# One conditioning pass behind each low part of weights, and four more pairs of tiles turned by transfers

## The chip, the cores and the metric

The kernel runs on one core of a Trainium2 chip. The time is the device time of one execution in microseconds (us); lower is better. The engines are named as in the profile: PE multiplies matrices (PEld is its weight load), DVE and ACT work element by element, POOL and SP here mostly issue transfers, and 16 DMA engines carry them.

## The reference

One decoder layer in float32, 256 tokens of width 2048, with two feed-forward parts around a token mixing:

```python
c_act = jax.nn.silu(c)
mod = (c_act @ w_ada[l] + b_ada[l]).reshape(b, N_MOD, D_MODEL)          # 9 x 2048
h = modulate(rms_norm(x, norm_ffn1[l]), mod[:, 0], mod[:, 1])
x = x + 0.5 * mod[:, 2][:, None, :] * swiglu(h, w_ffn1_gu[l], w_ffn1_down[l])
h = modulate(rms_norm(x, norm_mix[l]), mod[:, 3], mod[:, 4])
x = x + mod[:, 5][:, None, :] * token_mixing(h, w_in[l], w_ret_branch[l], w_swa_branch[l], w_out[l], sinks[l])
h = modulate(rms_norm(x, norm_ffn2[l]), mod[:, 6], mod[:, 7])
x = x + 0.5 * mod[:, 8][:, None, :] * swiglu(h, w_ffn2_gu[l], w_ffn2_down[l])
return rms_norm(x, norm_final)
```

`swiglu` multiplies by `w_gu` (2048 x 11264), forms silu(gate) * up (256 x 5632) and multiplies by `w_down`. `token_mixing` multiplies by `w_in` (2048 x 13312), runs a chunked retention and a sliding-window attention, multiplies each by a 2048 x 2048 branch matrix, gates and adds the two, and multiplies by `w_out` (2048 x 2048). The vector `mod` is the conditioning: a product of one row, c_act, with the whole of `w_ada` (2048 x 18432).

## The kernel before, in words

*Weights.* A matrix comes 1 MB at a time: `load` (L326) takes one of four buffers of the pool `raws` and issues the transfer on SP (L328). One such buffer holds two halves of 128 x 1024. `split` (L347) makes of each half a high part on ACT (L351, `wh`) and a low part on DVE (L353, `wl`), in a pool with three buffers of each. `products` (L331) then runs three matmuls for each of 4 column blocks of the activations: L338 high by high, L339 activations' low part by the weights' high part, L341 by the weights' low part. A low part is thus followed by 12 matmuls. In `gemm_part` (L390) each half ends with `tick()`, each 1 MB with `turn_step()`. L386 and L387 make high and low parts of activations in the same way.

*Conditioning.* The product with `w_ada` is done on DVE, not on PE: a row of 128 x 2048 (1 MB, `ada_load`, L201) is multiplied by silu(c) and summed in four passes of 512 columns (L206, `ada_pass`), each an instruction of DVE with a short one that reads the sum. `conditioning` (L243) is a generator that does one pass at each step, and issues a row's load some passes ahead (`pace["ahead"]`). `tick` advances it by `pace["rate"]` passes for each low part. The row sits in a buffer of `raws` too (`raw_row`) in the last group of the opening, in the mixing and in the second feed-forward part, and in half a slot (`two_rows`) in the rest of the first one. Three sets are done this way: 3 x 16 rows within the first feed-forward part, 3 x 16 within the mixing, 16 within the second feed-forward part.

*The opening.* The first 16 products of the first feed-forward part (pairs 0 to 7 of a gate and an up block) are done in four groups of inner blocks, L1009, while x is being normalised; in the last group each pair ends in `swiglu_up` (L657).

*Turning.* The result of a pair (two tiles of 128 x 512) must be transposed before the next product. `transpose_to` (L475) does it with four transposes on PE (L479) and a copy (L480, on ACT) for each tile. `turn_by_dma` (L486) does it without PE: two copies on ACT that lay the 16-bit halves apart (L496), a transposing transfer on SP (L501), two copies on ACT that put them together (L512); `later` (L613) spreads these over the next `turn_step`s.

*Order.* SP issues in the order of the program. On PE, DVE and ACT a scheduler orders the instructions by its own model of their times, except where the code is under a manual schedule. `tc.issue_after(ins)` forbids it to put an instruction ahead of `ins` on the same engine. `low[-1]` and `cast[-1]` are the newest low and high part, `pace["behind"]` is set by weights that are split by hand ahead of a stage (L469).

Of the kernel before, what the change touches and what calls it, by code (L numbers as in the profile page):

```python
# [20 lines left out]
DFF = 5632  # L21
# [3 lines left out]
CH = 512  # L25
# [3 lines left out]
EARLY = 8  # L29
# [48 lines left out]
def layer_kernel(  # L78
# [40 lines left out]
    def nm(s):  # L119
        uid[0] += 1  # L120
        return f"{s}_{uid[0]}"
# [16 lines left out]
    def slot():  # L138
        return slots.tile([P, KD * S], F32, tag="slot", name=nm("slot"))
# [55 lines left out]
    AQ = 4  # L195

    def ada_load(m, k, w, loads=1):
        src = w_ada[(m * KD + k) * P : (m * KD + k + 1) * P, :]
        for i in range(loads):
            at = slice(i * D // loads, (i + 1) * D // loads)  # L200
            nc.sync.dma_start(w[:, at], src[:, at])  # L201

    def ada_pass(k, w, sums, q, passes=AQ):

        at = slice(q * D // passes, (q + 1) * D // passes)
        nc.vector.tensor_tensor_reduce(  # L206
            out=w[:, at],
            in0=w[:, at],
            in1=cact[:, at],
            scale=1.0,  # L210
            scalar=0.0,
            op0=ALU.mult,
            op1=ALU.add,
            accum_out=sums[:, k, q : q + 1],
        )

    def ada_sums():
        return two.tile([P, KD, AQ], F32, tag="sums", name=nm("sums"))

    def ada_end(m, ks, sums, i=None, passes=AQ):  # L220

        dest = modc[:, m, ks]
        nc.vector.tensor_reduce(out=dest, in_=sums[:, ks, :passes], axis=AX.X, op=ALU.add)
        nc.vector.tensor_add(dest, dest, bcols[:, m, ks])
        if i is not None:
            nc.vector.tensor_mul(dest, dest, gains[:, i, ks])
# [16 lines left out]
    def conditioning(outputs, place, behind):  # L243


        tiles = [(m, k) for m, _, _ in outputs for k in range(KD)]
        held = {}
        step = 0
        for m, gain, row in outputs:
            sums = ada_sums()  # L250
            for k in range(KD):
                for q in range(AQ):
                    for i in range(step // AQ, min((step + pace["ahead"]) // AQ + 1, len(tiles))):
                        if i not in held:
                            held[i] = place()
                            ada_load(*tiles[i], held[i])
                    if behind is not None and step < 2 * AQ:
                        with tc.issue_after(behind.ins):
                            ada_pass(k, held[step // AQ], sums, q)
                    else:  # L260
                        ada_pass(k, held[step // AQ], sums, q)
                    step += 1
                    if k == KD - 1 and q == AQ - 1:
                        ada_end(m, slice(0, KD), sums, gain)
                        if row is not None:
                            gate_out(m, row)
                    yield

    def gate_out(m, row):

        ps = bank()
        nc.tensor.transpose(ps[:KD, :P], modc[:, m, :], ident)
        flat = t512()[:KD, :P]
        nc.scalar.mul(flat, ps[:KD, :P], row)
        nc.gpsimd.dma_start(gate_d[m // 3].rearrange("(k p) -> k p", p=P), flat)
# [6 lines left out]
    def gate_load(row, m):  # L282
        return nc.gpsimd.dma_start(row, gate_d[m // 3][None, :].broadcast_to([P, D]))
# [4 lines left out]
    def set_pace(outputs, halves, place, ahead):  # L288
        assert next(pace["steps"], None) is None
        pace["steps"] = conditioning(outputs, place, pace["behind"])  # L290
        pace["rate"] = len(outputs) * KD * AQ / halves
        pace["due"] = 0.0
        pace["ahead"] = ahead
# [9 lines left out]
    def turn_step():  # L303

        for one_turn in list(turns):
            if next(one_turn, turns) is turns:
                turns.remove(one_turn)
# [49 lines left out]
    cast, low, newest = [], [], []  # L357
# [49 lines left out]
    def gemm(act, w, col0s, KT=KD, ahead=None):  # L407
        banks = [[acc_bank() for _ in range(NT)] for _ in col0s]
        for kb in range(KT // KB):
            gemm_part(act, w, col0s, banks, kb, KT, None if kb else ahead)  # L410
            step()
        return banks
# [244 lines left out]
    def swiglu_up(banks_g, banks_u, tiles, ci, parts=None, by_dma=False):  # L657

        k0 = ci * KB
        dest = tiles[k0 // KD].rearrange("p (k s) -> p k s", s=S)  # L660
        kk = k0 % KD
        work = []
        for t in range(NT):
            s = t512()
            g, u = banks_g[t], banks_u[t]
            if parts is not None:
                nc.vector.tensor_add(s, g, parts[0][t])
                nc.vector.tensor_add(parts[1][t], u, parts[1][t])
                g, u = s, parts[1][t]
            nc.scalar.activation(s, g, AF.Silu)  # L670
            nc.vector.tensor_mul(s, s, u)  # L671
            if by_dma:
                work.append(turn_by_dma(dest[:, kk : kk + KB, t * P : (t + 1) * P], s))
                continue
            transpose_to(
                dest[:, kk : kk + KB, t * P : (t + 1) * P],
                lambda j: s[:, j * P : (j + 1) * P],
                KB,
            )
        if work:  # L680
            turns.append(later(work))

    def ffn_up(held, w, tiles, first, bg=None, turned=(), ahead=None):
        for ci in range(first, DFF // CH):
            bg = bg or gemm(held, w, [ci * CH])[0]
            bu = gemm(held, w, [DFF + ci * CH], ahead=ahead)[0]
            swiglu_up(bg, bu, tiles, ci, by_dma=ci in turned)
            bg = ahead = None
# [194 lines left out]
    gu, dn = w_ffn1_gu[0], w_ffn1_down[0]  # L883
    held = Held()
    part = [slot() for _ in range(3)]
    tiles = [slot(), part[0]]
# [3 lines left out]
    behind = [[back.tile([P, CH], F32, tag="back", name=nm("back")) for _ in range(NT)] for _ in range(2)]  # L890

    def part_of(n):
        if n < 2:
            return behind[n]
        if n >= 14:
            return [beside[n - 14][:, t, :] for t in range(NT)]
        at = ((n - 2) % 4) * NT * CH
        return [part[(n - 2) // 4][:, at + t * CH : at + (t + 1) * CH] for t in range(NT)]
# [7 lines left out]
    def place(m, k):  # L906
        if k < 1:
            rows_of[m, k] = raw_row()
        else:
            ring.append(ring.pop(0))  # L910
            rows_of[m, k] = ring[-1]
        ada_load(m, k, rows_of[m, k], 2 if k < 2 else 1)
# [80 lines left out]
    def to_parts(n):  # L993
        for p, b in zip(part_of(n), banks.pop(n)):
            if n in moved:
                nc.vector.tensor_add(p, p, b)  # L996
            else:
                nc.scalar.copy(p, b)
        moved.add(n)
# [9 lines left out]
    for g, ks in enumerate(groups):  # L1009
        final = g == len(groups) - 1  # L1010
        if final:
            set_pace(ROWS_FFN1, 32 * 192 // 32, place_row, 1)
        order = chunks if (len(groups) - g) % 2 else chunks[::-1]
        coming = iter(()) if final else group(groups[g + 1])
        due = 0 if final else 2 * len(groups[g + 1])
        stay = () if final else order[-2:]
        for i, n in enumerate(order):
            visit(n, ks, n not in stay, final)
            if final:
                turn_step()  # L1020
            last = len(order) - 2
            for _ in range((i + 1) * due // last - i * due // last if i < last else i == last):
                next(coming, None)
            if n in stay:
                continue
            if not final:
                to_parts(n)
            elif n % 2:
                swiglu_up(
                    banks.pop(n - 1),  # L1030
                    banks.pop(n),
                    tiles,
                    n // 2,
                    (part_of(n - 1), part_of(n)),
                    n // 2 in (1, 5),
                )
    gate = gate_row()
    tiles.append(slot())
    row_ring.append(two_rows())
    pace["rate"] = (192 - 32) / 117  # L1040
    pace["ahead"] = AQ
    ffn_up(held, gu, tiles, EARLY, turned=range(EARLY, DFF // CH - 1))
    gate_in = gate_load(gate, 2)
    wi = w_in[0]
    held, head, ahead, *calls = into_norm(3, wi, O_SK, O_SV)
# [336 lines left out]
    gate = gate_row()  # L1382
    tiles = [slot() for _ in range(3)]
    set_pace([(8, None, 0.5)], 160, raw_row, 2)
    ffn_up(held, w_ffn2_gu[0], tiles, 0, head, range(DFF // CH - 1), ahead)
    gf = one.tile([P, KD * S], F32, tag="hh", name="gf")[:, :D]
    spare = one.tile([P, 2, KD * P], F32R, tag="hl", name="spare")
    nc.gpsimd.dma_start(gf, norm_final[None, :].broadcast_to([P, D]))
# [107 lines left out]
```

## Time and profile before

| | us |
|---|---|
| median of three runs (lowest, highest) | 2388.58 (2387.45, 2389.75) |
| profiled execution | 2393.78 |
| its span, first to last instruction | 2392.0 |
| PE busy in it | 2351.4 (98%) |
| DVE busy | 1702.1 (71%) |
| ACT busy | 1310.0 (55%) |
| mean granted clock of TensorE | 0.997 |

Durations are read from the profiled execution. A group's row gives the line, the engine, the operation, what it writes and reads, how often, its busy time in us and the mean of one in ns, and the engine's idle time just before with what ended it. In the trace the passes of L206 are called CUSTOM_DVE_ANT_0, and the short instruction behind each DVE_READ_ACCUMULATOR2_ANT; in the order rows both are ISA. Names of buffers carry no numbers in the trace.

### The profile page before, as it was taken

Reading aid. Unit: us, or ns where it says so; the run is one execution under the profiler, and the core shown is the slowest. Engines: PE = TensorE matmul, PEld = TensorE weight load, DVE = VectorE, ACT = ScalarE, POOL = GpSimd, SP = SyncE. Lnnn points to the kernel's source line nnn. Section 1 sums busy time; section 2 is a strip of 40 time slices with the busy share of each in tenths; the row PEclk is TensorE's granted clock in tenths of the full one; section 3 lists DMA queues with packets and bytes.
Section 4 is the critical chain, followed back from the end, with each engine's and each line's share of the span. In section 5 each row is a group of like instructions: output and inputs, shape, how many; then the busy total and the mean of one; then the engine's idle time right before and its main releaser. Section 6 shows DMA issues by size and latency. Waiting matters only on the chain. (4 is left out here: it accounts for less than half of the span.)

```text
span 2392.0 us, 28418 instructions
## 1 busy us (share of the span) xinstructions
PE 2351.4 (98%) x10470; PEld 1924.5 (80%) x10470; DVE 1702.1 (71%) x2635; ACT 1310.0 (55%) x1792; POOL 7.7 (0%) x18
## 2 busy tenths in 40 slices
PE   7999999999999999999999999999999999999998
PEld 5788888888788888778887787887888888888886
DVE  6887799778877768976776676767655555545656
ACT  6553456454546568774555464466445445454544
POOL 0000000000000000000000000000000000000000
PEclk9999999999999999999999999999999999999999
DMA  9977789998876789867689797755667877765553
GB/s 354 367 278 277 265 284 342 349 339 316 321 255 236 279 270 247 253 213 286 248 278 293 236 299 282 272 195 192 237 238 237 254 247 246 255 220 194 183 204 124
DMA packets 177581, 625.78 MB, mean 262 GB/s; under 512 B 100321, under 2 KB 100705, under 8 KB 106913
## 3 DMA queue, kind: packets, MB, share of 16 engines
q1 hardware_dynamic: 175362, 613.11, 74.4%
q0 software_dynamic: 1504, 9.81, 1.0%
q8 instruction: 82, 1.34, 0.2%
q10 hardware_dynamic: 576, 1.05, 0.1%
q14 instruction: 57, 0.47, 0.1%
HBM read 597.16 MB, written 4.22 MB: 251 GB/s over the span
## 5 line engine op out<-in xcount | busy, mean ns | idle before, releaser
L351 ACT CAST wh<-raw 128x1024 fp32r<-128x1024 f32 x794 | 834.0, 1053 | 927.1 <-PE pa L339 895.4
L353 DVE TENSOR_TENSOR wl<-raw,wh 128x1024 fp32r<-128x1024 f32 x794 | 964.2, 1223 | 524.6 <-ACT wh L351 522.3
L338 PE MATMUL pa<-wh,hh 128*128 128x512 f32 x2192 | 855.4, 391 | 3.3 <-ACT wh L351 3.3
L339 PE MATMUL pa<-wh,hl 128*128 128x512 f32 x2192 | 854.5, 390 | 0.2 <-DVE hl L601 0.2
L341 PE MATMUL pa<-wl,hh 128*128 128x512 f32 x2192 | 778.2, 392 | 1.4 <-DVE wl L353 1.3
L338 PEld LDWEIGHTS pa<-wh,hh 128*128 128x128 f32 x2192 | 411.9, 188 | 93.6 <-ACT wh L351 5.3
L341 PEld LDWEIGHTS pa<-wl,hh 128*128 128x128 f32 x2192 | 409.9, 188 | 90.4 <-DVE wl L353 4.3
L339 PEld LDWEIGHTS pa<-wh,hl 128*128 128x128 f32 x2192 | 412.1, 188 | 85.2 <-DVE hl L601 0.4
L339 PE MATMUL pa<-wh,a 128*128 128x512 f32 x944 | 365.8, 390 | 0.4 <-DVE a L387 0.4
L341 PE MATMUL pa<-wl,a 128*128 128x512 f32 x944 | 351.0, 392 | 9.4 <-DVE wl L353 9.4
L338 PE MATMUL pa<-wh,a 128*128 128x512 f32 x944 | 350.7, 392 | 1.7 <-DVE t L607 1.1
L206 DVE CUSTOM_DVE_ANT_0 raw<-raw,cact 128x512 f32<-128x512 f32 (+1 forms) x296 | 189.8, 695 | 65.5 <-DMA raw<-in_w_ada_dram 59.4
L341 PEld LDWEIGHTS pa<-wl,a 128*128 128x128 f32 x944 | 177.3, 188 | 49.9 <-DVE wl L353 13.5
L338 PEld LDWEIGHTS pa<-wh,a 128*128 128x128 f32 x944 | 178.0, 189 | 40.3 <-DVE t L607 1.9
L339 PEld LDWEIGHTS pa<-wh,a 128*128 128x128 f32 x944 | 177.8, 188 | 37.9 <-DVE a L387 1.0
L206 DVE CUSTOM_DVE_ANT_0 slot<-slot,cact 128x512 f32<-128x512 f32 (+1 forms) x216 | 170.0, 835 | 5.1 <-DMA slot<-in_w_ada_dram 4.8
L512 ACT COPY slot<-back 128x512 uint16<-128x512 uint16 x124 | 82.7, 766 | 0.0
L387 DVE TENSOR_TENSOR a<-slot,a 128x512 fp32r<-128x512 f32 x118 | 80.5, 684 | 0.0
L386 ACT CAST a<-slot 128x512 fp32r<-128x512 f32 x118 | 72.7, 617 | 1.9 <-DVE t L671 1.9
L496 ACT COPY flat<-t 128x512 uint16<-128x512 uint16 x112 | 63.5, 616 | 8.1 <-DVE t L1344 5.5
L206 DVE DVE_READ_ACCUMULATOR2_ANT sums<- 128x1 f32 x512 | 42.2, 82 | 0.0
L996 DVE TENSOR_TENSOR slot<-slot,pa 128x512 f32<-128x512 f32 x48 | 31.9, 683 | 3.2 <-PE pa L341 3.1
(205 smaller groups left out, 1143.1 us busy)
## 6 DMA issues: line engine op xcount, KB each, us to landing
raw<-in_w_ffn_gu_dram SPq DMA_DIRECT2D x160, 1024.0 KB, 5.2
raw<-in_w_in_dram SPq DMA_DIRECT2D x104, 1024.0 KB, 5.7
raw<-in_w_ffn_down_dram SPq DMA_DIRECT2D x88, 1024.0 KB, 4.9
raw<-in_w_ada_dram SPq DMA_DIRECT2D x73, 1024.0 KB, 5.5
slot<-in_w_ada_dram SPq DMA_DIRECT2D x67, 1024.0 KB, 7.1
raw<-in_w_ffn_gu_dram SPq DMA_DIRECT2D x32, 512.0 KB, 5.5
raw<-in_w_swa_branch_dram SPq DMA_DIRECT2D x16, 1024.0 KB, 5.1
raw<-in_w_ret_branch_dram SPq DMA_DIRECT2D x16, 1024.0 KB, 5.0
```

The source lines that it names most:

```text
L206: nc.vector.tensor_tensor_reduce(out=w[:, at], in0=w[:, at], in1=cact[:, at], scale=1.0, scalar=0.0, op0=ALU.mult, op1=ALU.add, accum_out= ...
L338: nc.tensor.matmul(ps, ah[:, j, ts], wh[:, j, :], start=first, stop=False)
L339: nc.tensor.matmul(ps, al[:, j, ts], wh[:, j, :], start=False, stop=False)
L341: nc.tensor.matmul(ps, ah[:, j, ts], wl[:, j, :], start=False, stop=last).ins
L351: cast.append(nc.scalar.copy(hi, src).ins)
L353: low.append(nc.vector.tensor_sub(lo, src, hi.bitcast(F32)).ins)
L386: nc.scalar.copy(hi, v)
L387: nc.vector.tensor_sub(lo, v, hi.bitcast(F32))
L496: nc.scalar.copy(planes[:, i, :], words(src)[:, :, i])
L512: nc.scalar.copy(into[:, :, :, i], held["turned"][:, i])
L996: nc.vector.tensor_add(p, p, b)
```

## The change

Each pass that isn't one of a stage's first eight is now bound to stand behind the newest low part at the point where `tick` asks for it. In the opening the pairs 1, 3, 5 and 7 are turned by transfers, where 1 and 5 were; in both feed-forward parts the last chunk, number 10, is turned by transfers too. From L257 on, the lines of the changed kernel have numbers lower by two (L351 becomes L349, L353 L351, L479 L477).

```diff
-                    if behind is not None and step < 2 * AQ:
-                        with tc.issue_after(behind.ins):
-                            ada_pass(k, held[step // AQ], sums, q)
-                    else:
+                    at_start = behind is not None and step < 2 * AQ
+                    with tc.issue_after(behind.ins if at_start else low[-1]):
                         ada_pass(k, held[step // AQ], sums, q)
...
                     (part_of(n - 1), part_of(n)),
-                    n // 2 in (1, 5),
+                    n // 2 % 2 == 1,
                 )
...
-    ffn_up(held, gu, tiles, EARLY, turned=range(EARLY, DFF // CH - 1))
+    ffn_up(held, gu, tiles, EARLY, turned=range(EARLY, DFF // CH))
...
-    ffn_up(held, w_ffn2_gu[0], tiles, 0, head, range(DFF // CH - 1), ahead)
+    ffn_up(held, w_ffn2_gu[0], tiles, 0, head, range(DFF // CH), ahead)
```

Counted over the program: PE has 40 transposes of L479 where it had 72, ACT 16 more copies of L496, 16 more of L512 and 8 fewer of L480, SP eight more transposing transfers and otherwise the same order. DVE has the same passes and low parts.

The first place is DVE in the last group of the opening. Before, the four passes of the first row in `raws` (`raw_2352`) stand together:

```order
330 L353 TENSOR_TENSOR wl_2286<-raw_2281,wh_2285 128x1024
331 L353 TENSOR_TENSOR wl_2302<-raw_2281,wh_2301 128x1024
332 L206 ISA raw_2352,sums_2351<-raw_2352,cact 128x512
333 L206 ISA sums_2351 128x1
334 L206 ISA raw_2352,sums_2351<-raw_2352,cact 128x512
335 L206 ISA sums_2351 128x1
336 L206 ISA raw_2352,sums_2351<-raw_2352,cact 128x512
337 L206 ISA sums_2351 128x1
338 L206 ISA raw_2352,sums_2351<-raw_2352,cact 128x512
339 L206 ISA sums_2351 128x1
340 L353 TENSOR_TENSOR wl_2318<-raw_2283,wh_2317 128x1024
```

Now the first of them stands behind two more low parts, and the next behind one each:

```order
331 L351 TENSOR_TENSOR wl_2302<-raw_2281,wh_2301 128x1024
332 L351 TENSOR_TENSOR wl_2318<-raw_2283,wh_2317 128x1024
333 L599 TENSOR_TENSOR hl_125<-t_2264,hh_124 128x256
334 L351 TENSOR_TENSOR wl_2336<-raw_2333,wh_2335 128x1024
335 L206 ISA raw_2352,sums_2351<-raw_2352,cact 128x512
336 L206 ISA sums_2351 128x1
337 L351 TENSOR_TENSOR wl_2356<-raw_2333,wh_2355 128x1024
338 L206 ISA raw_2352,sums_2351<-raw_2352,cact 128x512
339 L206 ISA sums_2351 128x1
```

The passes of one row moved from between two low parts to behind four different ones.

The second place is DVE late in the mixing, in the first branch product. A buffer's number grows in the order of the program, so that a row with a number above that of the weights beside it is one asked for later. Before:

```order
1828 L353 TENSOR_TENSOR wl_11152<-raw_11149,wh_11151 128x1024
1829 L206 ISA raw_11207,sums_10735<-raw_11207,cact 128x512
1830 L206 ISA sums_10735 128x1
1831 L206 ISA raw_11207,sums_10735<-raw_11207,cact 128x512
1832 L206 ISA sums_10735 128x1
1833 L206 ISA raw_11207,sums_10735<-raw_11207,cact 128x512
1834 L206 ISA sums_10735 128x1
1835 L206 ISA raw_11207,sums_10735<-raw_11207,cact 128x512
1836 L206 ISA sums_10735 128x1
1837 L353 TENSOR_TENSOR wl_11169<-raw_11149,wh_11168 128x1024
1838 L353 TENSOR_TENSOR wl_11192<-raw_11189,wh_11191 128x1024
```

And now, at the same low part of the program (its numbers are higher by six):

```order
1823 L351 TENSOR_TENSOR wl_11158<-raw_11155,wh_11157 128x1024
1824 L206 ISA raw_11131,sums_10741<-raw_11131,cact 128x512
1825 L206 ISA sums_10741 128x1
1826 L351 TENSOR_TENSOR wl_11175<-raw_11155,wh_11174 128x1024
1827 L206 ISA raw_11131,sums_10741<-raw_11131,cact 128x512
1828 L206 ISA sums_10741 128x1
1829 L351 TENSOR_TENSOR wl_11198<-raw_11195,wh_11197 128x1024
1830 L206 ISA raw_11131,sums_10741<-raw_11131,cact 128x512
```

Before, the row stood ahead of weights that the program asks for earlier (`raw_11189`), and so behind fewer low parts since its load; now the pass at this place reads an older row, `raw_11131`, and one pass stands behind each low part.

The third place is ACT at the end of the first feed-forward part's up products. Before, pair 10 is copied from PSUM after PE's transposes:

```order
346 L512 COPY slot_3129<-back_4051 128x4x128 x2
347 L512 COPY slot_3129<-back_4091 128x4x128 x2
348 L351 CAST wh_4212<-raw_4210 128x1024
349 L480 COPY slot_3129<-ps_4096 128x4x128
350 L480 COPY slot_3129<-ps_4105 128x4x128
351 L351 CAST wh_4229<-raw_4210 128x1024
```

Now its tiles are laid apart for the transfers:

```order
349 L510 COPY slot_3115<-back_4055 128x4x128 x2
350 L510 COPY slot_3115<-back_4095 128x4x128 x2
351 L494 COPY flat_4196<-t_4097 128x512 x2
352 L384 CAST a_4199<-slot_129 128x512
353 L349 CAST wh_4207<-raw_4205 128x1024
354 L349 CAST wh_4224<-raw_4205 128x1024
355 L494 COPY flat_4242<-t_4100 128x512 x2
```

Two copies of a whole tile became four of its halves, spread between the casts of the following product, and four more that put the halves together come later.

## The prediction

> **What bounds the kernel now.** I read the page's busy row and its groups first, then the list of waits, then 60 us windows over the whole span, and last the timeline of the windows that stood out. The busy row and groups of the page:
>
> ```profile
> PE 2351.4 (98%) x10470; PEld 1924.5 (80%) x10470; DVE 1702.1 (71%) x2635; ACT 1310.0 (55%) x1792; POOL 7.7 (0%) x18
> L351 ACT CAST wh<-raw 128x1024 fp32r<-128x1024 f32 x794 | 834.0, 1053 | 927.1 <-PE pa L339 895.4
> L353 DVE TENSOR_TENSOR wl<-raw,wh 128x1024 fp32r<-128x1024 f32 x794 | 964.2, 1223 | 524.6 <-ACT wh L351 522.3
> ...
> L206 DVE CUSTOM_DVE_ANT_0 raw<-raw,cact 128x512 f32<-128x512 f32 (+1 forms) x296 | 189.8, 695 | 65.5 <-DMA raw<-in_w_ada_dram 59.4
> ```
>
> PE is busy 98% of the span: what can be won is PE's stops and PE's own work. ACT's casts stand 895 us waiting for PE to give a high part back, so ACT is ahead of PE in general. A conditioning pass (L206) is the only frequent DVE work that waits for a transfer: 59.4 us. The waits, of the whole span and then (last row) of 1260 to 1400 us alone:
>
> ```profile
> DVE raw L206 <- DMA raw<-in_w_ada_dram: 59.4, 37, 3.3
> PE pa L341 <- DVE wl L353: 11.4, 14, 2.2
> PE pa L341 <- DVE wl L353: 6.7, 6, 2.2
> ```
>
> More than half of PE's waits for a low part lie in 140 us. The windows give time, PE busy (matmuls), PEld, DVE, ACT, POOL, the granted clock, the DMA share and GB/s:
>
> ```profile
> 1260.00:1320.00 60.00, 57.57 (x250) 46.36 (x249) 41.11 (x70) 37.22 (x49) 0.00 (x0) 1.00 1.00 291
> 1320.00:1380.00 60.00, 54.94 (x224) 43.84 (x224) 43.77 (x74) 26.24 (x32) 0.00 (x0) 0.94 0.71 250
> 1380.00:1440.00 60.00, 60.00 (x266) 49.67 (x266) 45.00 (x73) 36.74 (x46) 0.00 (x0) 1.00 0.89 285
> 1440.00:1500.00 60.00, 58.17 (x257) 47.82 (x256) 38.98 (x64) 25.84 (x29) 0.00 (x0) 1.00 0.79 294
> 1500.00:1560.00 60.00, 59.45 (x262) 48.50 (x261) 42.22 (x63) 28.91 (x34) 1.05 (x2) 1.00 0.73 260
> ```
>
> A full window holds 266 matmuls, one per 60/266 = 0.2256 us. The others lack 16, 42, 9 and 4: 71 matmuls, 16.0 us. How one such loss comes about, in the timeline (start, length, then what it waited for):
>
> ```profile
> 1319.12 0.69 DVE L206 CUSTOM_DVE_ANT_0 raw<-raw,cact 128x512 f32<-128x512 f32 x1 [2.67 <-DMA raw<-in_w_ada_dram]
> ...
> 1319.73 0.69 DVE L206 CUSTOM_DVE_ANT_0 raw<-raw,cact 128x512 f32<-128x512 f32 x1
> ...
> 1320.96 0.69 DVE L206 CUSTOM_DVE_ANT_0 raw<-raw,cact 128x512 f32<-128x512 f32 x1
> ...
> 1321.57 1.22 DVE L353 TENSOR_TENSOR wl<-raw,wh 128x1024 fp32r<-128x1024 f32 x1
> ...
> 1322.85 0.72 PE L341 MATMUL pa<-wl,a 128*128 128x512 f32 x2 [2.18 <-DVE wl L353]
> ```
>
> DVE stands 2.67 us in front of a row that has not landed, does its four passes back to back (0.61 us apart, 2.45 us in all), and only then the low part that PE needs: 5.1 us on a queue of which PE has at most about 3.1 us in stock (three high and low parts, of which two are worth 2 x 12 x 0.2256 = 5.4 us, less the 2.3 us that a cast and a low part take by the groups above). PE stands 2.18 us, and the clock follows:
>
> ```profile
> 1320.00:1325.00 5.00, 2.82 (x9) 1.92 (x9) 4.53 (x9) 0.18 (x1) 0.00 (x0) 0.85 0.85 305
> 1325.00:1330.00 5.00, 5.00 (x19) 4.03 (x18) 1.83 (x2) 2.47 (x3) 0.00 (x0) 0.81 0.73 277
> 1360.00:1365.00 5.00, 4.14 (x11) 3.31 (x12) 2.54 (x3) 0.89 (x1) 0.00 (x0) 0.66 0.85 285
> ```
>
> The granted clock lacks (0.15 + 0.19 + 0.34) x 5 = 3.4 us of full speed after two such stops; the 16.0 us contain that.
>
> **The change, part by part.** *The passes.* No pass is added or taken away; each moves. In the order rows of the final opening group and of the mixing tail, four passes of a row stand between two low parts before, and one behind each low part now, three to ten low parts later. So where a row was reached 2.67 us before it landed, three low parts of 12 x 0.2256 = 2.71 us, 8.1 us, now lie between: the wait goes, and the longest piece of passes ahead of a low part falls from 2.45 to 0.61 us, well inside the stock of 3.1 us. I credit the whole 16.0 us of the windows (both ends: 8, if only the half that stands in the waits of 1260 to 1400 us, 6.7 us and its clock, follows the passes; 16.0 if all does), and 1 us of the waits outside 1260 to 1400 us (11.4 less 6.7, of which part stands in the two last windows already). What is late next: the pass itself, at no cost; a set's last pass moves by about nine low parts, 24 us, and no wait of the trace of before has PE standing for conditioning (L206) that this could lengthen.
>
> *What moves with them: buffers.* The transfer queue's order of loads is as before but for the added transposes. A load waits until the buffer four places back is free, and rows share the four buffers with weights:
>
> ```profile
> SPq L328 <- DVE wl L353: 1014.5, 242, 10.5
> SPq L328 <- DVE sums L206: 125.3, 55, 4.1
> ```
>
> SP stands for a free buffer almost always, so what frees it sets when a transfer starts. A row that is passed over later is held longer. Counting releases in the two orders, a row's load had one to three low parts between its release and its first use before, and has five to eleven now; a weight's load had five or seven, and has three over low parts 383 to 530 (mixing and its output product), and in the opening over 101 to 132 and 283 to 310. With three, two buffers carry the weights: in the time of four low parts (10.83 us) must fit landing, cast 1.05, low part 1.22, pass 0.61, low part 1.22, together landing + 4.1 us.
>
> ```profile
> raw<-in_w_ffn_gu_dram SPq DMA_DIRECT2D x160, 1024.0 KB, 5.2
> raw<-in_w_in_dram SPq DMA_DIRECT2D x104, 1024.0 KB, 5.7
> ...
> slot<-in_w_ada_dram SPq DMA_DIRECT2D x67, 1024.0 KB, 7.1
> raw<-in_w_ffn_gu_dram SPq DMA_DIRECT2D x32, 512.0 KB, 5.5
> raw<-in_w_swa_branch_dram SPq DMA_DIRECT2D x16, 1024.0 KB, 5.1
> ...
> back<-flat SPq DMA_TRANSPOSE x62, 6.6
> ```
>
> At 5.1 to 5.7 us the loop takes 9.2 to 9.8 us: it closes with 1.0 to 1.6 us over. Single late loads will still be seen; I take 1.5 us lost, from 0 to the case of rival one.
>
> *DVE in the opening.* There DVE has no room:
>
> ```profile
> 320.00:360.00 40.00, 40.00 (x186) 33.22 (x185) 37.14 (x61) 22.06 (x29) 0.00 (x0) 1.00 0.93 291
> 360.00:400.00 40.00, 39.60 (x184) 32.24 (x183) 37.24 (x71) 25.62 (x35) 0.00 (x0) 1.00 0.96 314
> ```
>
> It is busy 37.1 of 40 us, and the DMA engines 93 to 96%. The same passes, spread out, leave nothing to catch up with. 0 to 6 us; I take 2, nearer to the low end since PE is full (40.00, 39.60) with the bursts in.
>
> *The turned pairs.* Pairs 3 and 7 of the opening and the last chunk of both feed-forward parts leave PE: 8 times 4 transposes. A group of eight as the timeline has it:
>
> ```profile
> 526.51 0.40 PE L341 MATMUL pa<-wl,a 128*128 128x512 f32 x1
> 526.75 1.04 PE L479 MATMUL ps<-small_c,t 128*128 128x128 f32 x8
> 527.54 0.48 PE L338 MATMUL pa<-wh,a 128*128 128x512 f32 x1
> ```
>
> From 526.75 to 527.54 is 0.79 us, and 0.1 us more till matmuls run at their pace: 0.89 us, four times, 3.6 us off PE, which is the path. Nothing covers for it, so all of it counts. ACT gains work:
>
> ```profile
> L512 ACT COPY slot<-back 128x512 uint16<-128x512 uint16 x124 | 82.7, 766 | 0.0
> ...
> L496 ACT COPY flat<-t 128x512 uint16<-128x512 uint16 x112 | 63.5, 616 | 8.1 <-DVE t L1344 5.5
> ...
> L480 ACT COPY slot<-ps 128x512 f32<-128x512 f32 x18 | 10.0, 583 | 1.4 <-PE ps L479 1.4
> ```
>
> 16 x 0.616 + 16 x 0.766 - 8 x 0.583 = 17.4 us, in pieces of 1.2 to 1.5 us between casts. ACT's 895 us of waiting for PE hide them, and ACT is busy 25.6 of 40 us where the opening's two are added; if that cover were gone each of the 16 pieces would cost its length, 22 us. I take nothing.
>
> *Eight more transfers.* Each turns 128 x 1024 two-byte words, 256 KB. Its DMA time has no row. The hardware queue moves 613.11 MB in 74.4% of the span, 2.9 us a MB, which for 256 KB gives 0.76 us; above it stands the 6.6 us to landing. Four of them fall into the opening, where 4 to 7% of DMA time is free: 0 to 4 us, and I take 1.5. The Trainium skill (Advanced Engine Details and Errata, X-Bar Transpose (TRN2)) says that transposing DMAs are as fast as ordinary ones; by that this term would be 0.7 and the sum 0.8 us lower. This trace does not agree so far as it shows it: 256 KB take 6.6 us to landing, and 1 MB of weights 5.2.
>
> **The sum.** -16.0 - 1 - 3.6 + 1.5 + 2 + 1.5 = -15.6 us on the profiled execution's 2393.8 us. That execution stands 5.2 us above the median of the runs, 2388.6, with the same kernel; taken from the median, 2373.0 us. With every loss at nothing: -21, 2367.
>
> **Rivals.** One, slower: two weight buffers are not enough. In the stretches with three low parts of lead (208 low parts, 52 loops) the loop of landing + 4.1 us passes 10.83 us as soon as a weight takes over 6.7 us to land. At the 7.1 us of the slot rows it lacks 0.4 us each time, 21 us; with 0.3 us more, where a weight and a row are let go by neighbouring low parts and share the engines, 36 us. Against the 20.6 won and 3.5 of other losses that makes +4 to +19, 2393 to 2408; it decides from about 7.1 us to landing (17.1 us lost over 52 loops, 0.33 each). For it: DVE and the DMA engines are full in the opening, and every transfer that SP holds is let go by a release. Against it: medians of 5.1 to 5.7 us, and PE's stock of 3.1 us swallows single late loads. The Trainium skill (Perfetto Trace Analysis, Identifying Performance Opportunities) says that a gap which repeats on the engine that should be full can mean too few buffers for the next tile; no such repeating gap stands in the trace of before.
>
> Two, half: the waits for rows go, but casts late for other reasons (turning copies ahead of a cast, a DMA share of 1.00 in 1260 to 1320 us) keep half of the 16.0: -8 - 1 - 3.6 + 5 = -7.6, 2381.
>
> Three, no change: the low parts are late in the tail whatever the passes do, and only the transposes are won, against 1.5 to 3.5 us of losses: -2 to 0, 2387 to 2389. Against it: DVE's 2.67 us of standing and its four passes lie directly ahead of the late low part.
>
> **The numbers.** The forecast 0.55, rival two 0.13, three 0.11, one 0.21. This kernel's runs can tell about 0.2% (4.8 us) from no change, so faster has 0.68, the same 0.11, slower 0.21. The range reaches from the sum without losses, 2367, to 2398, a third into rival one; what is left outside is most of that rival's chance, some 0.14, and 0.04 below. The forecast's own range, where the tail's credit holds and the losses stay within their ends, is 2367 to 2380.
>
> **What will show it.** Right: DVE's wait for rows in raw falls from 59.4 us to under 10; PE's wait of L341 for low parts from 11.4 to under 4; the windows from 1260 to 1560 us hold 264 or more matmuls each and a clock of 1.00; PE's transposes of L479 fall by 32 matmuls; the opening's PE busy stays at 39 of 40 us. Wrong: casts that wait for weights (ACT wh for DMA raw, in many places), matmul counts below 260 in windows between 1060 and 1560 us, or in 300 to 400 us; then rival one holds. Counts as low as before at the same places, with passes no longer next to them, would show rival three.

## The result and the profile after

The changed kernel takes 2546.83 us (median of 4 runs, 2545.7 to 2550.29) beside 2388.18 of the kernel before: a ratio of 1.0666, 95% interval 1.0647 to 1.0684. It is slower by 159 us, where 15.6 us less was forecast and the stated range ended at 2398.

First the busy row of its page, two groups and the clock, to be held against those shown of before:

```profile
PE 2399.9 (94%) x10438; PEld 1941.6 (76%) x10438; DVE 1704.8 (67%) x2636; ACT 1318.9 (52%) x1815; POOL 7.7 (0%) x18
...
PEclk9999999888898999999999999999999999999999
...
L349 ACT CAST wh<-raw 128x1024 fp32r<-128x1024 f32 x794 | 827.5, 1052 | 1031.6 <-PE pa L337 685.4
...
L206 DVE CUSTOM_DVE_ANT_0 raw<-raw,cact 128x512 f32<-128x512 f32 (+1 forms) x296 | 203.5, 691 | 9.0 <-ACT cact L173 6.0
```

What the change was to do to DVE it did: the passes on rows in raws no longer wait for transfers. PE lost its 98%, and its clock fell in a stretch from about 420 to 860 us. The windows there, in the order of columns as before:

```profile
300.00:360.00 60.00, 60.00 (x275) 49.61 (x274) 55.64 (x96) 35.86 (x45) 0.00 (x0) 1.00 0.75 275
360.00:420.00 60.00, 55.94 (x253) 45.46 (x250) 45.43 (x80) 33.84 (x48) 0.00 (x0) 0.99 0.80 280
420.00:480.00 60.00, 45.05 (x167) 35.16 (x168) 33.31 (x62) 23.19 (x28) 0.00 (x0) 0.84 0.61 218
480.00:540.00 60.00, 43.55 (x162) 33.90 (x161) 27.38 (x51) 19.28 (x25) 2.23 (x4) 0.83 0.62 226
...
780.00:840.00 60.00, 48.21 (x184) 36.33 (x182) 34.26 (x61) 20.79 (x24) 0.00 (x0) 0.91 0.55 213
840.00:900.00 60.00, 53.83 (x224) 43.63 (x224) 45.21 (x62) 33.53 (x39) 0.00 (x0) 0.94 0.76 290
900.00:960.00 60.00, 60.00 (x282) 49.75 (x281) 41.32 (x77) 33.26 (x60) 1.09 (x2) 1.00 0.52 201
```

PE, DVE, ACT and the DMA engines all have room there at once, so none of them is full; a queue that stands would look like this. The lag puts a number on it. It is the time at which a given low part ends, less the time at which the same low part ends in the first profile of before:

| low part | 100 | 120 | 140 | 160 | 200 | 240 | 300 | 380 | 440 | 540 | 820 |
|---|---|---|---|---|---|---|---|---|---|---|---|
| before, us | 306 | 366 | 421 | 475 | 585 | 696 | 862 | 1108 | 1289 | 1578 | 2343 |
| lag of the change, us | -0.6 | -4.5 | 7.7 | 38.9 | 100.6 | 156.2 | 155.7 | 164.8 | 161.6 | 153.0 | 151.8 |

From low part 120 to 240, the rest of the first feed-forward part behind the opening, 160.7 us are lost; everywhere else together 9 are won. In that stretch rows lie not in raws but in the two halves of one slot (`two_rows`). The transfer queue's waits from 420 to 840 us, of before (first three rows) and of the change:

```profile
SPq L328 <- DVE wl L353: 266.5, 61, 6.5
...
SPq L328 <- DVE sums L206: 7.5, 4, 2.7
...
SPq L201 <- DVE sums L206: 4.9, 3, 2.0
```

```profile
SPq L201 <- DVE sums L206: 362.8, 34, 14.1
SPq L326 <- ACT wh L349: 1.4, 4, 0.4
```

Before, SP mostly stood at loads of weights until a buffer came free (L328); a row's passes were done together as soon as they could be, and SP stood only 4.9 us for one of them at a row's load. Now it stands 362.8 of 420 us at the load of a row (L201), waiting for a pass; a load of weights finds its buffer free when its turn comes. One such turn in the timeline, first SP, then DVE, then ACT and PE:

```profile
602.73 0.33 SPq L201 DMA_DIRECT2D slot<-in_w_ada_dram  x1
603.17 0.84 SPq L326 DMA_DIRECT2D raw<-in_w_ffn_down_dram  x2
616.10 0.33 SPq L201 DMA_DIRECT2D slot<-in_w_ada_dram  x1
616.53 0.37 SPq L326 DMA_DIRECT2D raw<-in_w_ffn_down_dram  x1
```

```profile
614.24 1.22 DVE L351 TENSOR_TENSOR wl<-raw,wh 128x1024 fp32r<-128x1024 f32 x1
615.38 0.68 DVE L206 CUSTOM_DVE_ANT_0 slot<-slot,cact 128x512 f32<-128x512 f32 x1
```

```profile
610.80 1.99 ACT L349 CAST wh<-raw 128x1024 fp32r<-128x1024 f32 x2 [7.46 <-DMA raw<-in_w_ffn_down_dram]
...
611.90 0.79 PE L336 MATMUL pa<-wh,a 128*128 128x512 f32 x1 [4.22 <-ACT wh L349]
```

The pass that frees a half stands behind a low part and ends at 616.06. The row's load goes out at 616.10, and the weights behind it in the queue only then, at 616.53. They are wanted at once: of the pair sent at 603.17 the first was there for ACT's cast at 610.8, for which ACT had stood 7.46 us and PE then 4.22. The circle is closed: the pass waits for a low part, the low part for weights, the weights for their place behind a row's load, and that for the pass before.

Windows of 420 to 840 us hold 1211 matmuls where seven full ones hold 1862: 147 us. PE stood idle 97 us of that. The other 50 were lost while it was busy: the granted clock was 0.88 in the mean, which over the 323 us of busy PE would make 39 us, an estimate. What took the remaining 11 isn't shown.

### The profile page after: what moved, and what is told of

Read it like the earlier page. It is cut to its first block, busy times and chain, and to the rows that moved or that the text cites. A ratio compares the mean times of both kernels' runs of the same rounds, so it can differ in the third digit from the quotient of the medians.

```text
span 2544.2 us, 28349 instructions
## 1 busy us (share of the span) xinstructions
PE 2399.9 (94%) x10438; PEld 1941.6 (76%) x10438; DVE 1704.8 (67%) x2636; ACT 1318.9 (52%) x1815; POOL 7.7 (0%) x18
## 3 DMA queue, kind: packets, MB, share of 16 engines
q10 hardware_dynamic: 576, 1.05, 0.1%
HBM read 597.16 MB, written 4.22 MB: 236 GB/s over the span
## 4 chain that ended last, share of the span: by engine, by line
PE 46%; DMA 3%; DVE 2%; issue 1%; ACT 1%; SPq 0%; DVEq 0%; ACTq 0%
PE pa L336 15%; PE pa L339 15%; PE pa L337 15%; DMA raw<-in_w_in_dram 1%; DMA raw<-in_w_ret_branch_dram 1%; DVE wl L351 1%; ACT wh L349 1%; DMA raw<-in_w_swa_branch_dram 1%; DVE raw L206 0%; SPq L499 0%; PE ps L1191 0%; PE pd L1288 0%; PE pd L1275 0%; PE pd L1290 0%; PE pd L1289 0%
## 5 line engine op out<-in xcount | busy, mean ns | idle before, releaser
L351 DVE TENSOR_TENSOR wl<-raw,wh 128x1024 fp32r<-128x1024 f32 x794 | 968.2, 1222 | 706.8 <-ACT wh L349 703.0
L349 ACT CAST wh<-raw 128x1024 fp32r<-128x1024 f32 x794 | 827.5, 1052 | 1031.6 <-PE pa L337 685.4
L336 PE MATMUL pa<-wh,hh 128*128 128x512 f32 x2192 | 864.5, 396 | 47.1 <-ACT wh L349 47.1
L339 PE MATMUL pa<-wl,hh 128*128 128x512 f32 x2192 | 787.3, 394 | 4.2 <-DVE wl L351 3.7
L336 PE MATMUL pa<-wh,a 128*128 128x512 f32 x944 | 365.0, 403 | 54.6 <-ACT wh L349 54.6
L337 PE MATMUL pa<-wh,a 128*128 128x512 f32 x944 | 377.9, 401 | 12.6 <-DVE a L385 12.4
L336 PEld LDWEIGHTS pa<-wh,a 128*128 128x128 f32 x944 | 183.0, 194 | 101.4 <-ACT wh L349 62.6
L337 PEld LDWEIGHTS pa<-wh,a 128*128 128x128 f32 x944 | 183.0, 194 | 58.2 <-DVE a L385 20.2
L206 DVE CUSTOM_DVE_ANT_0 raw<-raw,cact 128x512 f32<-128x512 f32 (+1 forms) x296 | 203.5, 691 | 9.0 <-ACT cact L173 6.0
L510 ACT COPY slot<-back 128x512 uint16<-128x512 uint16 x140 | 93.3, 766 | 0.0
L494 ACT COPY flat<-t 128x512 uint16<-128x512 uint16 x128 | 72.4, 617 | 2.3 <-DVE t L1263 2.2
```

What stands on the lines that cost most here:

```text
L206: nc.vector.tensor_tensor_reduce(out=w[:, at], in0=w[:, at], in1=cact[:, at], scale=1.0, scalar=0.0, op0=ALU.mult, op1=ALU.add, accum_out= ...
L336: nc.tensor.matmul(ps, ah[:, j, ts], wh[:, j, :], start=first, stop=False)
L337: nc.tensor.matmul(ps, al[:, j, ts], wh[:, j, :], start=False, stop=False)
L339: nc.tensor.matmul(ps, ah[:, j, ts], wl[:, j, :], start=False, stop=last).ins
L349: cast.append(nc.scalar.copy(hi, src).ins)
L351: low.append(nc.vector.tensor_sub(lo, src, hi.bitcast(F32)).ins)
```

## The experiments

The first five ask whether the transfer queue is the cause, and whether anything else is lost in this stretch. Some of these kernels have a few more lines, so that L204, L329 or L352 stands where the kernel before has L201, L328 or L351.

**The ring's passes left free.** `pin` is false from the end of the opening to the mixing.

```diff
-                    with tc.issue_after(behind.ins if at_start else low[-1]):
+                    if at_start or pace["pin"]:
+                        with tc.issue_after(behind.ins if at_start else low[-1]):
+                            ada_pass(k, held[step // AQ], sums, q)
+                    else:
                         ada_pass(k, held[step // AQ], sums, q)
```

> The change as it is, but while rows lie in the slot ring (the rest of the first feed-forward part after the opening) the passes are left to the scheduler, as before. Theory A, the transfer queue: there a row's load waits for the last pass of the row two before it in the ring, that pass now stands behind a late low part, and the weights queued behind the load on SP wait too; the lag of 161 us between low parts 120 and 240 is all of the loss, so this run gives 2380 to 2392 us. Theory B, the loss comes from the new transposing transfers or from the four buffers of raws: it stays above 2480 us.

Measured: 2392.93 us beside 2386.08, ratio 1.0028 (1.0018 to 1.0037). 154 of the 159 us are gone. It ends 0.9 us above the range: between low parts 120 and 240 the lag still rises by 12 us, from -5.4 to 6.9, so that this run doesn't give all of the 161 us to the ring's passes.

**Only the ring's passes bound,** in the kernel before.

> The kernel before, with passes bound behind the newest low part only while rows lie in the slot ring; pairs turned as before. Theory A: this part alone makes the loss, 2540 to 2556 us. Theory B: under 2470 us.

Measured: 2534.33 us, ratio 1.0620 (1.0604 to 1.0635), a little under the range. This one stretch, without the new turned pairs, makes 148 us, and the lag rises by 152 us between low parts 120 and 240.

**The rows' loads on another queue,** all passes still bound.

```diff
+            queue = nc.gpsimd if row_ring_on else nc.sync
-            nc.sync.dma_start(w[:, at], src[:, at])
+            queue.dma_start(w[:, at], src[:, at])
```

> The change as it is, but the loads of rows into the slot ring are issued from POOL's queue instead of SP's, so that no weight stands behind them; the passes stay bound. Theory A: the row still waits for its half of the ring but blocks no weight, and the lag between low parts 120 and 240 falls from 161 to under 20 us, 2380 to 2405 us. Rival C, the ring of two rows is itself too short, so that DVE stands at passes for rows that land late, and the low parts behind them: above 2450 us.

Measured: 2392.0 us, ratio 1.0027 (1.0010 to 1.0044). The lag rises by 5 us from low part 120 to 240 (from -3.1, over 4.1 at 140, to 1.7). The passes are bound as in the change, 149 of them stand between these two low parts in both, and rows still wait for their half, now on POOL; only no weight stands behind them. The queue is the cause, and the ring is not too short. POOL's waits for a pass over the whole span, then SP's for buffers of weights from 420 to 840 us:

```profile
POOL slot L204 <- DVE sums L209: 277.7, 33, 43.9
```

```profile
SPq L329 <- DVE wl L354: 287.6, 64, 6.9
```

**A row's load later in the queue.** `pace["ahead"] = 0` in the ring.

> The change as it is, but in the ring a row's load is put in the transfer queue at the row's own first pass, not four passes ahead of it. Between the pass that frees a half and the load that waits for it then lie 5 passes of the program instead of 1, 3.7 low parts or 9.9 us instead of 0.7 or 2.0 us. Theory A: the weights behind it get that lead, the loss goes nearly all: 2380 to 2405 us. Rival C: rows are asked for later, so DVE stands at them longer: at or above 2546 us.

Measured: 2399.69 us, ratio 1.0052 (1.0037 to 1.0067). Asking for a row later made the kernel 147 us faster than the change as it is. The lag rises 11 us between low parts 140 and 160 and is level from there on; at that place a transposing transfer held SP for 11.87 us, and ACT then stood 14.57 us for the weights behind it:

```profile
460.46 11.87 SPq L499 DMA_TRANSPOSE back<-flat  x1
472.38 2.44 SPq L326 DMA_DIRECT2D raw<-in_w_ffn_gu_dram  x1
```

```profile
478.66 1.99 ACT L349 CAST wh<-raw 128x1024 fp32r<-128x1024 f32 x2 [14.57 <-DMA raw<-in_w_ffn_gu_dram]
```

In this run SP still stood 220.4 us for passes at rows' loads from 420 to 840 us (362.8 in the change). So a long stand of the queue isn't by itself the loss. What counts is whether the weights behind it still land in time.

**One step between.** `pace["ahead"] = 3`, to see how the loss grows with the room that is lacking.

> The change as it is, with a ring row's load put three passes ahead of its own first pass in the transfer queue, where it is four. Between the pass that frees a half and the load that waits for it lie 2 passes, 1.5 low parts or 4.0 us; it is 1 pass or 2.0 us with four ahead (about 160 us lost over 40 rows, 4.0 us a row) and 9.9 us with none ahead (about 11 us lost). Theory: a weight behind that load needs about 6 us of room, and what is lacking is lost once a row, 6 less 4 or 2 us: 80 us, 2455 to 2480 us. Rival: the loss is there whenever the load is asked for ahead of the row's passes at all, 2540 us, or gone as soon as more than one pass lies between, under 2410 us.

Measured: 2476.33 us, ratio 1.0373 (1.0353 to 1.0393). The lag rises by 89.5 us from low part 120 to 240, 2.2 us a row where 2 were expected. With 2.0, 4.0 and 9.9 us of room the rows cost 4.0, 2.2 and 0.3 us each: what lacks to about 6 us is lost once a row. The 6 us were read off the change itself, and the 0.3 is mostly the one held transfer above; the run with 4.0 us of room is the test, and it came out within its range.

The next five ask where the forecast's 15.6 us went, with the ring's stretch out of the way. They compare with the kernel before: each is that kernel with one part of the change, or that kernel itself.

**Only the four pairs turned.**

> The kernel before, with the four more pairs turned by transfers and no pass bound. Theory: 3.6 us of transposes leave PE, and 1 to 2 us come back where the new transfers delay loads in the opening, so 2383 to 2386 us beside a before of 2386 to 2388. Rival: eight more transfers in SP's queue and 17 us of copies on ACT cost more than the transposes did, above 2389 us, with the lag rising between low parts 100 and 160.

Measured: 2386.73 us beside 2385.88, ratio 1.0005 (0.9994 to 1.0016): -1.4 to +3.8 us, no difference that can be told. Neither the 2 us forecast nor the rival's loss is shown. In its profile the lag goes from 1.2 at the start over -3.9 at low part 120 to 0.0 at 400, and falls 1.1 from 540 to 820; but between 440 and 500, where its order is that of before, it falls by 8 us. That puts the profile of before itself in question.

**The kernel before, profiled again.**

> The kernel before, profiled once more. Between 1260 and 1560 us the first profile lacked 71 matmuls of full windows (16.0 us), at a granted clock of 0.94 in one window; two later kernels with the same code in that stretch lacked some 30. Theory: the two stops that brought the clock down belong to that one execution, so this one lacks 25 to 40 matmuls (6 to 9 us) at a clock of 1.00. Rival: the loss is the kernel's own, 60 to 75 matmuls again.

Measured: 2387.57 us, where the first profiled execution took 2393.78. The windows from 1260 us:

```profile
1260.00:1320.00 60.00, 58.78 (x257) 47.83 (x257) 41.97 (x72) 38.07 (x50) 0.00 (x0) 1.00 0.96 297
1320.00:1380.00 60.00, 57.69 (x252) 46.83 (x251) 47.14 (x78) 29.07 (x35) 0.00 (x0) 1.00 0.76 272
1380.00:1440.00 60.00, 60.00 (x267) 49.69 (x266) 43.15 (x70) 36.77 (x46) 0.00 (x0) 1.00 0.90 297
1440.00:1500.00 60.00, 58.38 (x255) 47.21 (x254) 42.04 (x74) 26.53 (x30) 0.00 (x0) 1.00 0.74 277
1500.00:1560.00 60.00, 59.46 (x261) 48.46 (x261) 40.25 (x56) 28.19 (x34) 1.05 (x2) 1.00 0.72 258
```

They lack 9, 14, 0, 11 and 5 matmuls: 39, 8.8 us, at full clock. The first profile's 71 include the two stops after which the clock fell. Some 7 of the 16.0 us that the forecast credited were that one execution's. Against the first profile this one's lag falls by 6.6 us between low parts 440 and 500, so that every lag against the first holds a fall of about this size that isn't the run's own. The 4 us that the change wins in the table behind low part 240 are no gain of it.

**Passes bound in the mixing only,** and then **only from the end of its softmax stage.**

> The kernel before, with passes bound behind the newest low part in all of the mixing and nowhere else; pairs turned as before. In the runs so far the lag against before rises by about 7 us between low parts 300 and 380 (where softmax runs beside the w_in products, with casts that wait for w_in weights 71 us where it was 4) and falls by about 12 between 380 and 530. Theory: both belong to the bound passes of the mixing, so -5, 2381 to 2385 us. Rival: the rise comes from elsewhere (state carried over from the first feed-forward part): -12, 2374 to 2378 us.

> The kernel before, with passes bound only from the end of the softmax stage to the end of the mixing; pairs turned as before. Theory: a row in raws is held by its bound passes, for 16 low parts at the softmax stage's rate of 0.25 passes a low part, which leaves weights two buffers there; without that stage the rise goes and the fall of 12 us stays: 2374 to 2379 us. Rival: the fall belongs to the earlier stage's passes having been done late: 2384 us or more.

Measured: 2391.45 us, ratio 1.0019 (1.0006 to 1.0032), and 2385.93 us, ratio 0.9997 (0.9988 to 1.0006), beside 2385.88. The first lies above the ranges of its theory and of its rival, the second in the range of its rival. The fall of about 12 us that both theories counted on was for the most part the first profile's: the unchanged kernel, profiled again, falls by 6.6 there. Between the two runs, the softmax stage's bound passes cost 5.5 us in the medians, near the 7 expected, and a lag that rises from -0.6 to 9.7 between low parts 300 and 380 (level at 1.3 without them). ACT's waits for weights, from 880 to 1120 us, passes bound in all of the mixing and then only from the end of the softmax stage:

```profile
ACT wh L352 <- DMA raw<-in_w_in_dram: 37.3, 12, 5.2
```

```profile
ACT wh L352 <- DMA raw<-in_w_in_dram: 4.0, 1, 4.0
```

The casts stand longer for weights. That rows, passed over at every fourth low part, keep two of the four buffers of raws there is counted from the program; no row of the trace shows it. In the tail the exchange is even. From 1260 to 1560 us, the second profile of before, then the tail bound:

```profile
DVE raw L206 <- DMA raw<-in_w_ada_dram: 23.7, 15, 3.2
...
PE pa L341 <- DVE wl L353: 4.7, 5, 1.6
```

```profile
ACT wh L352 <- DMA raw<-in_w_in_dram: 31.7, 11, 5.2
ACT wh L352 <- DMA raw<-in_w_swa_branch_dram: 20.1, 7, 6.1
ACT wh L352 <- DMA raw<-in_w_ret_branch_dram: 7.5, 5, 2.4
...
PE pa L340 <- DVE a L388: 2.5, 6, 1.3
...
PE pa L339 <- ACT wh L352: 1.7, 3, 1.0
```

DVE's 23.7 us of standing for rows are gone, and ACT stands 59.3 us for weights where no such row was in the list. The tail bound lacks 35 matmuls in these five windows, 7.9 us: 0.9 less than the 8.8 of before, one profile against one.

**Passes bound in the opening only.**

> The kernel before, with passes bound only in the last group of the opening; pairs turned as before. In the runs so far the lag falls by 4 to 5 us to low part 120 and rises by 5 to 12 to low part 140. Theory: rows held back in raws must all be passed as the opening ends, loads of weights and of the first ring rows come late together, so the fall is paid back: -1 to +3, 2385 to 2390 us. Rival: the rise comes from the transfers that turn pairs 3 and 7, so without them the fall of about 3 us stays: 2383 to 2385 us.

Measured: 2387.68 us, ratio 1.0013 (1.0004 to 1.0021). The lag falls from 1.5 to -2.2 at low part 120 and is 2.0 at 140: what is won is paid back as the opening ends. Half of the fall isn't the bound passes' own: the second profile of before falls by 1.9 there.

**A version of the parts that did not cost:** the pairs turned, ring rows on POOL's queue with their passes bound, the mixing bound from the end of the softmax stage, the rest free.

> A version put together from the parts that did not cost: the four more pairs turned by transfers; rows of the ring loaded from POOL's queue, their passes bound; passes bound in the mixing only from the end of the softmax stage; the opening's last group, the mixing up to there and the second feed-forward part left to the scheduler. Theory: about 2 us from the pairs, 2 to 4 from the ring's stretch, 0 to 3 from the mixing's end: 2378 to 2383 us beside a before of 2386. Rival: each of these is within what runs differ by, so 2384 to 2388 us.

Measured: 2381.74 us beside 2386.99, ratio 0.9984 (0.9970 to 0.9998). It lies in the range of its theory and is faster than both kernels, but against the kernel before barely so: the interval reaches from 0.5 to 7 us, and its weaker end lies in the rival's range.

## Why the prediction was wrong

*The step that failed* is the count of buffers. It looked at raws alone, "the buffer four places back", and found a lead of three low parts for weights. The passes also free the halves of the ring, and there the lead was a single pass, 2.0 us. The term for late loads was set at 1.5 us, with raws in it and the ring not; the ring's passes alone cost 148 us. The text said that each load waits on SP for a release, and it quoted the row that shows SP always standing; it did not ask, for the load of a ring row, who stands behind it. With that lead put in the forecast's own loop, a loss was to be seen, though not its size. As an estimate: landing 5.2, cast 1.05, low part 1.22 and pass 0.68 come one after another once a row, 8.2 us against 7.9 us of PE work a row (2.9 low parts), so 0.3 us a row are lost at the least. Measured were 4.0. From 420 to 840 us of the change the weights took longer to land than the 5.2 of the page, and with these times the same loop is 10.1 to 10.6 us:

```profile
raw<-in_w_ffn_down_dram SPq DMA_DIRECT2D x32, 1024.0 KB, 7.6
raw<-in_w_ffn_gu_dram SPq DMA_DIRECT2D x17, 1024.0 KB, 7.1
```

The one row that pointed there, the ring's loads with 7.1 us to landing, was used for its time alone.

*The credit of 16.0 us* was mis-sized twice. A second profile of before has 8.8 us there, and with the passes bound in the tail the profile has 7.9, at the same median time. The mechanism shown in the timeline (a row not landed, four passes, a late low part) was real; what was late next was not the pass, "at no cost", but the weights, whose buffers the later pass holds.

*Rival one* named a loss of the right kind, weights that are released too late, and its sign came: casts wait for weights in many places (105.6 us for w_gu, 103.4 for w_down). Its places were wrong. In the low parts 383 to 530, where it counted most of its 21 to 36 us, the exchange is even; the softmax stage before them, which it did not name, lost 5.5, and the ring, which it did not count, 148. The Trainium skill's sentence on repeating gaps (Perfetto Trace Analysis, Identifying Performance Opportunities) fits the profile of the change, where PE stops 24 times for a high part between 420 and 840 us, 89.6 us in all. It gives too few buffers as a possible reason; here the two buffers of the ring were enough as soon as no weight stood behind them.

*What held:* no transpose came back, 32 matmuls of L479 fewer on PE; DVE's waits for rows in raws went below 10 us. In the change the five windows of the tail, 150 us later, hold 264, 249, 265, 260 and 264 matmuls at a clock of 1.00: two are still below the 264 that the prediction set as a sign of being right. The turned pairs' 3.6 less 1.5 us lie just outside the interval of their run, which ends at a gain of 1.4, so that this gain isn't shown, nor can the cost of the 17 us of copies be told apart in it. A slip of the sum: 16.0, 1 and 3.6 us without losses lead to 2368, not 2367.

## What to carry to other kernels

An instruction that is moved later also frees its buffer later. List every buffer that it frees, find the transfer that waits for each, and ask what stands behind that transfer in its queue: in a queue that keeps its order, as SP's does here, a transfer asked for early but released late blocks all others. Where that is so, ask for it later or from another queue. A stop that is to be credited should be seen in two executions: here 7 of 16 us were those of a single one.

## What was not expected of the hardware

PE's granted clock can fall after a stop of about 2 us, and need not, so that two stops of one length can have different prices. In before's first profile a stop of 2.18 us was followed by windows of 0.85 and 0.81, and one of 2.04 us by a window of 0.66. With passes bound in the opening only, a stop of 2.43 us left the clock at 1.00, in its own window of 5 us as in the one before it and the three behind it:

```profile
1485.00:1490.00 5.00, 2.59 (x12) 1.82 (x10) 3.71 (x10) 1.06 (x1) 0.00 (x0) 1.00 0.52 187
```

What decides between the two isn't shown here. The Trainium skill (TensorE: Matmul & The Clock Gate, Part 1: The HAM clock gate) names about 3.4 us of idleness for the drop; the 2.18 and 2.04 us here were fewer.

A transposing transfer of 256 KB can hold SP for long, with every load behind it: the median of a profile's 62 to 70 issues was 1.24 to 1.39 us, but every profile has some over 4 us, and the longest was 11.87. Why isn't shown.
